# Two of four sums of weight blocks formed by adding transfers, and more pairs of k-tiles in seven block products

## Chip, cores and metric

The kernel runs on one core of one Trainium2 chip. The metric is the device time of one execution in microseconds (us). Three runs of the kernel before took 2425.48, 2425.89 and 2425.93 us; the median, 2425.89, is the time before.

## The reference, cut to what matters

A decoder trunk of two layers works on a residual stream x of 256 tokens by 2048, in float32. Layer 0 mixes tokens by retention in 8 heads, layer 1 by latent attention in 16 heads, and a SwiGLU network of width 5632 follows each. Every sub-layer is `x = x + rms_norm(f(rms_norm(x)))`.

```python
def swiglu(x, w_gu, w_down):
    gate, up = jnp.split(x @ w_gu, [D_FF], axis=-1)
    return (jax.nn.silu(gate) * up) @ w_down

for i in range(DEPTH):
    h = rms_norm(x, norm_mix_pre[i])
    h = retention(h, ...) if i % 2 == 0 else mla(h, ...)
    x = x + rms_norm(h, norm_mix_post[i])
    h = rms_norm(x, norm_ffn_pre[i])
    x = x + rms_norm(swiglu(h, ffn_w_gu[i], ffn_w_down[i]), norm_ffn_post[i])
```

Nearly all the work is the products of 256 tokens with large weight matrices, which are read from memory once.

## The kernel before

**Products.** A k-tile is 128 rows of a weight matrix. A group (`group`) forms 256 tokens by 1024 output columns in four PSUM banks: two token tiles t by two column halves c of 512. Its loop runs over the k-tiles: 16 in the retention's input projection (4 groups of q and k, named rqk, and 8 of v and gate, rvg) and in the gate/up projection (11 groups in each of two layers, gu); the down projection (dn, 44 k-tiles), the retention's output (rto, 32) and the attention's output (mlo, 16) have two groups each, called halves, in `closing`.

**Precision.** Each float32 operand is split (`split`) into a rounded part hi, a cast on ACT (line 203), and a rest lo, a subtraction on DVE (line 204). A product is three matmuls: hi by hi, hi by lo, lo by hi. So an ordinary pair of k-tiles has 2 tiles x 2 t x 2 c x 3 = 24 matmuls of 512 columns.

**Seven products.** For the pairs named in GU_SEVENS, DN_SEVENS, RTO_SEVENS and RET_SEVENS the four blocks of the pair's weights (two k-tiles by two halves, b00, b01 in the first tile and b10, b11 in the second) and the four blocks of activations are multiplied in Strassen's way (Winograd's form): seven products in place of eight, so 21 matmuls in place of 24 (`seven`). They need four sums of activation blocks (`left_sums`, made once and used by all groups of a stage) and four sums of weight blocks, made for each pair in each group (`right_sums`, lines 246 to 249):

    t1 = b00 + b01     t3 = b01 + b11     t2 = t1 + b11     t4 = t2 + b10

Each is an addition of 512 columns on DVE. The sums t1 and t3 lie in the tile ta, t2 and t4 in tb; both are split like weights. b01 itself isn't split, since no product uses it alone. After the last seven of a group, `combine` takes four products out of four extra banks, and `add` adds them to the group's banks.

**What sets the order.** The program is written in the order of the loops, and a scheduler puts each engine's instructions in an order of its own when the program is built; on the chip each engine keeps that order and waits at an instruction until its operands and its buffer are there. A tile with a tag has as many buffers as `bufs` says: raw weights (`raw`) four, hi and lo (`whi`, `wlo`) five each. A buffer is given to the next tile when the last reader of the old one has finished: whi and wlo are freed by PE, raw by DVE. All weights are loaded by SP's queue, 512 KB for a k-tile. `later` and `step` put small pieces of work (transposes, norms) a number of k-tiles ahead in the next group; in gate/up two sets of four transposes stand between pair 0 and pair 1, and ACT copies their results to aT.

Of the kernel before, what the change touches and what calls it, by code (L numbers as in the profile page):

```python
# [33 lines left out]
GU_SEVENS = (2, 3, 5)  # L34
DN_SEVENS = (2, 5, 8, 11, 14, 17)
RTO_SEVENS = (2, 6, 10)
RET_SEVENS = (2, 4)
# [19 lines left out]
def trunk(  # L57
# [153 lines left out]
    def weights(load, parts, name):  # L211

        raw = wp.tile([P, 1024], F32, tag="raw", bufs=RAW, name=f"{name}_raw")
        load(raw)
        hi = wp.tile([P, 1024], F32R, tag="whi", bufs=WB, name=f"{name}_hi")
        lo = wp.tile([P, 1024], F32R, tag="wlo", bufs=WB, name=f"{name}_lo")
        for a, n, g in parts:
            split(hi[:, a : a + n], lo[:, a : a + n], raw[:, a : a + n], g)
        return hi, lo, raw
# [18 lines left out]
    def right_sums(raw0, raw1, name):  # L238

        b00, b01 = raw0[:, 0:512], raw0[:, 512:1024]  # L240
        b10, b11 = raw1[:, 0:512], raw1[:, 512:1024]
        res = {}
        ta = tp7.tile([P, 1024], F32, tag="tsum", bufs=2, name=f"{name}_ta")
        tb = tp7.tile([P, 1024], F32, tag="tsum", bufs=2, name=f"{name}_tb")
        t1, t3, t2, t4 = ta[:, 0:512], ta[:, 512:1024], tb[:, 0:512], tb[:, 512:1024]
        nc.vector.tensor_add(out=t1, in0=b00, in1=b01)
        nc.vector.tensor_add(out=t3, in0=b01, in1=b11)
        nc.vector.tensor_add(out=t2, in0=t1, in1=b11)
        nc.vector.tensor_add(out=t4, in0=t2, in1=b10)  # L249
        for both, src, n in ((ta, (1, 3), "a"), (tb, (2, 4), "b")):  # L250
            hi = wp.tile([P, 1024], F32R, tag="whi", bufs=WB, name=f"{name}_t{n}hi")
            lo = wp.tile([P, 1024], F32R, tag="wlo", bufs=WB, name=f"{name}_t{n}lo")
            split(hi, lo, both)
            for i, k in enumerate(src):
                sl = slice(i * 512, (i + 1) * 512)
                res[k] = hi[:, sl], lo[:, sl]
        return res

    def group(
        lhs, kts, load, name, lead=2, skew=0, tail=0, banks=None, between=None, sevens=(), left=None  # L260
    ):

# [50 lines left out]
        def seven(p, final):  # L313
            k0, k1 = 2 * p, 2 * p + 1

            def b(kt, c):
                return lambda: tuple(x[:, c * 512 : (c + 1) * 512] for x in w[kt][:2])
# [13 lines left out]
        def combine():  # L331
            def kept(n):
                return wp.tile([P, 512], F32, tag="mv", bufs=3, name=f"{name}_mv{n}")

            m1, u, v = kept(0), kept(1), kept(2)
# [4 lines left out]
            x = tp7.tile([P, 1024], F32, tag="tsum", bufs=2, name=f"{name}_mx")[:, 0:512]  # L340
# [65 lines left out]
    def tile_load(w, g, name, halves=0):  # L406
# [3 lines left out]
        def load(kt, first_half=False):  # L410
            n = 512 if kt < halves or first_half else 1024

            def dma(raw):
                for a in range(0, 1024, 512 if kt < halves else 1024):
                    m = 512 if kt < halves else 1024
                    nc.sync.dma_start(out=raw[:, a : a + m], in_=w[g, kt, :, a : a + m])

            parts = [(a, n, None) for a in range(0, 512 if first_half else 1024, n)]
            return weights(dma, parts, f"{name}_w{kt}")
# [6 lines left out]
    hT = hp.tile([P, DT, 2, NT, P], F32R, tag="hT", name="hT")  # L426
# [4 lines left out]
    def watched(sevens, tiles):  # L431

        made, held = {}, {}

        def seen(t, k0, n, part):
            for p in sevens:
                if k0 <= 2 * p < k0 + n:
                    held[t, p] = part[:, 2 * p - k0], part[:, 2 * p - k0 + 1]
                    if (1 - t, p) in held:
                        f, hi, lo = tiles(len(made))  # L440
# [4 lines left out]
        return made  # L445

    def norm_piece(t, i, ssq, col):
# [6 lines left out]
        ks = slice(k0, k0 + n)  # L454
        part = wp.tile([P, 512], F32, tag="mv", bufs=3, name=f"hx{t}{i}")
# [5 lines left out]
        split(hT[:, ks, 0, t, :], hT[:, ks, 1, t, :], part)  # L461
# [11 lines left out]
    def h_lhs(kt, t, c):  # L473
        return hT[:, kt, 0, t, :], hT[:, kt, 1, t, :]

    rx_next = [None] * NT

# [13 lines left out]
    yg = sb.tile([P, NT, D], F32, tag="yg", name="yg")  # L491

    def closing(act, kts, w, g_post, col, name, skew=4, sevens=(), sums=None):


        last = col is None
        ssq = [small(4, "ssq", 4, f"{name}_ssq{t}") for t in range(NT)]
# [3 lines left out]
        def parted(half, b):  # L501
# [5 lines left out]
            if b in sevens:  # L507
# [4 lines left out]
        def update(t, k0, n):  # L512
            sl = slice(k0 * P, (k0 + n) * P)
            nc.vector.scalar_tensor_tensor(
                out=xs[:, t, sl], in0=yg[:, t, sl], scalar=r[t], in1=xs[:, t, sl],
# [13 lines left out]
        parted(0, 0)  # L529
        for half in range(2):  # L530
            gp = sb.tile([P, 1024], F32, tag="gp", name=f"{name}_gp")
            nc.sync.dma_start(
                out=gp, in_=g_post[half * 1024 : (half + 1) * 1024].partition_broadcast(P)
            )

# [6 lines left out]
            def load(kt, *first_half):  # L542
# [5 lines left out]
                return slices(kt, *first_half)  # L548
# [21 lines left out]
            def scaled(banks, t):  # L570
                for c in range(2):
                    col = half * 2 + c
                    nc.vector.tensor_tensor(  # L573
                        out=yg[:, t, col * 512 : (col + 1) * 512], in0=banks[t][c],
                        in1=gp[:, c * 512 : (c + 1) * 512], op=ALU.mult,
                    )

            def first_done(banks):
# [10 lines left out]
                lhs, kts, load, f"{name}{half}", skew=skew if half else 0, tail=2 if half else 0,  # L589
# [632 lines left out]
```

## Time and profile before

| What | Value |
|---|---|
| profiled execution, its time | 2426.96 us |
| its span | 2425.2 us |
| mean granted TensorE clock | 0.998 |
| bytes moved, mean rate | 463.78 MB, 191 GB/s |
| a rqk group, and a gate/up group, on PE | 46.59 us, 42.70 us |
| 1024-column cast on ACT, subtraction on DVE | 1.05 us, 1.22 us |

The span is the time from the first to the last instruction. The page of the profile gives each engine's busy time, the DMA queues and the chain of work that ended last; views of the trace give instructions grouped by line, waits, issues of transfers with their time to landing, and timelines. In a row of instructions, `gu_w_lo<-gu_w_raw,gu_w_hi` names the tile written and the tiles read. The time of an instruction includes the tail in which its writes are confirmed; the next one on its engine starts before that.

### The profile page before, as it was taken

Reading aid. Unit: us, or ns where it says so; the run is one execution under the profiler, and the core shown is the slowest. Engines: PE = TensorE matmul, PEld = TensorE weight load, DVE = VectorE, ACT = ScalarE, POOL = GpSimd, SP = SyncE. Lnnn points to the kernel's source line nnn. Section 1 sums busy time; section 2 is a strip of 40 time slices with the busy share of each in tenths; the row PEclk is TensorE's granted clock in tenths of the full one; section 3 lists DMA queues with packets and bytes.
Section 4 is the critical chain, followed back from the end, with each engine's and each line's share of the span. In section 5 each row is a group of like instructions: output and inputs, shape, how many; then the busy total and the mean of one; then the engine's idle time right before and its main releaser. Section 6 shows DMA issues by size and latency. Waiting matters only on the chain.

```text
span 2425.2 us, 30883 instructions
## 1 busy us (share of the span) xinstructions
PE 2412.2 (99%) x10972; PEld 1993.3 (82%) x10972; DVE 2080.2 (86%) x2865; ACT 1409.8 (58%) x1882; POOL 26.2 (1%) x38
## 2 busy tenths in 40 slices
PE   9999999999999999999999999999999999999998
PEld 7888888888888888888888888888888888888886
DVE  7888888888878998888999997876889889899997
ACT  5454555555656655555565665655655565556664
POOL 0000000000000000000000000000000000000000
PEclk9999999999999999999999999999999999999999
DMA  7556556555665565666656655336556656566654
GB/s 255 173 194 194 180 184 200 171 190 191 198 212 189 183 206 190 199 204 191 203 190 209 207 198 163 123 132 199 184 182 202 197 192 212 183 204 199 204 198 162
DMA packets 129612, 463.78 MB, mean 191 GB/s; under 512 B 14640, under 2 KB 15024, under 8 KB 129456
## 3 DMA queue, kind: packets, MB, share of 16 engines
q1 hardware_dynamic: 129456, 461.80, 58.5%
q8 instruction: 86, 1.41, 0.2%
q14 instruction: 70, 0.57, 0.1%
HBM read 459.64 MB, written 2.10 MB: 190 GB/s over the span
## 4 chain that ended last, share of the span: by engine, by line
PE 96%; DVE 2%; DMA 1%; issue 1%; ACT 0%; SPq 0%; DVEq 0%; POOLq 0%; POOL 0%; ACTq 0%
PE gu_b L399 31%; PE dn_b L399 14%; PE rvg_b L399 12%; PE gu_m L399 7%; PE rto_b L399 6%; PE rqk_b L399 6%; PE mlo_b L399 4%; PE q L399 3%; PE dn_m L399 2%; PE rvg_m L399 2%; PE mc_b L399 2%; PE ftp L816 1%; PE rqk_m L399 1%; PE rto_m L399 1%; PE ry L749 1%; PE htp L451 1%
## 5 line engine op out<-in xcount | busy, mean ns | idle before, releaser
L399 PE MATMUL gu_b<-gu_w_hi,hT 128*128 128x512 f32 x1976 | 564.0, 392 | 0.0
L203 ACT CAST gu_w_hi<-gu_w_raw 128x1024 fp32r<-128x1024 f32 (+1 forms) x352 | 342.4, 979 | 238.2 <-PE gu_b L399 163.8
L204 DVE TENSOR_TENSOR gu_w_lo<-gu_w_raw,gu_w_hi 128x1024 fp32r<-128x1024 f32 (+1 forms) x352 | 392.3, 1130 | 47.4 <-ACT gu_w_hi L203 45.4
L399 PEld LDWEIGHTS gu_b<-gu_w_hi,hT 128*128 128x128 f32 x1976 | 366.7, 188 | 75.0 <-DVE hT L204 0.9
L399 PE MATMUL gu_b<-gu_w_lo,hT 128*128 128x512 f32 x988 | 310.1, 390 | 0.0
L203 ACT CAST dn_w_hi<-dn_w_raw 128x1024 fp32r<-128x1024 f32 (+1 forms) x176 | 172.8, 993 | 99.6 <-DMA dn_w_raw<-w_down 51.9
L399 PE MATMUL rvg_b<-rvg_w_hi,hT 128*128 128x512 f32 x800 | 227.0, 391 | 0.0
L399 PEld LDWEIGHTS gu_b<-gu_w_lo,hT 128*128 128x128 f32 x988 | 185.2, 188 | 39.5 <-DVE gu_w_lo L204 0.6
L204 DVE TENSOR_TENSOR dn_w_lo<-dn_w_raw,dn_w_hi 128x1024 fp32r<-128x1024 f32 (+1 forms) x176 | 196.3, 1148 | 8.6 <-ACT dn_w_hi L203 7.9
L203 ACT CAST rvg_w_hi<-rvg_w_raw 128x1024 fp32r<-128x1024 f32 (+1 forms) x128 | 127.3, 1000 | 117.6 <-PE rvg_b L399 93.6
L204 DVE TENSOR_TENSOR rvg_w_lo<-rvg_w_raw,rvg_w_hi 128x1024 fp32r<-128x1024 f32 (+1 forms) x128 | 145.2, 1154 | 36.1 <-ACT rvg_w_hi L203 34.9
L399 PEld LDWEIGHTS rvg_b<-rvg_w_hi,hT 128*128 128x128 f32 x800 | 149.0, 188 | 30.3
L399 PE MATMUL dn_b<-dn_w_hi,dn_ah 128*128 128x512 f32 x536 | 169.7, 390 | 0.1
L399 PE MATMUL dn_b<-dn_w_lo,dn_ah 128*128 128x512 f32 x536 | 169.0, 389 | 0.0
L399 PE MATMUL dn_b<-dn_w_hi,dn_al 128*128 128x512 f32 x536 | 168.9, 389 | 0.0
L399 PE MATMUL rvg_b<-rvg_w_lo,hT 128*128 128x512 f32 x400 | 124.8, 390 | 0.0
L399 PE MATMUL rqk_b<-rqk_w_hi,hT 128*128 128x512 f32 x428 | 121.0, 394 | 1.1 <-ACT rqk_w_hi L203 0.9
L399 PEld LDWEIGHTS dn_b<-dn_w_hi,dn_al 128*128 128x128 f32 x536 | 100.6, 188 | 20.9
L399 PEld LDWEIGHTS dn_b<-dn_w_lo,dn_ah 128*128 128x128 f32 x536 | 100.6, 188 | 20.9
L399 PEld LDWEIGHTS dn_b<-dn_w_hi,dn_ah 128*128 128x128 f32 x536 | 100.3, 188 | 21.0 <-DVE yg L573 0.4
L203 ACT CAST gu_w_tbhi<-gu_w_tb 128x1024 fp32r<-128x1024 f32 x60 | 63.1, 1052 | 86.7 <-DVE gu_w_tb L249 47.4
L204 DVE TENSOR_TENSOR gu_w_tblo<-gu_w_tb,gu_w_tbhi 128x1024 fp32r<-128x1024 f32 x60 | 73.5, 1225 | 36.8 <-ACT gu_w_tbhi L203 34.3
(442 smaller groups left out, 4763.9 us busy)
## 6 DMA issues: line engine op xcount, KB each, us to landing
gu_w_raw<-w_gu SPq DMA_DIRECT2D x352, 512.0 KB, 4.3
dn_w_raw<-w_down SPq DMA_DIRECT2D x176, 512.0 KB, 4.4
rvg_w_raw<-ret_vg SPq DMA_DIRECT2D x128, 512.0 KB, 4.4
rto_w_raw<-ret_out SPq DMA_DIRECT2D x64, 512.0 KB, 4.4
rqk_w_raw<-ret_qk SPq DMA_DIRECT2D x63, 512.0 KB, 4.4
mlo_w_raw<-mla_out SPq DMA_DIRECT2D x32, 512.0 KB, 3.5
uq_w_raw<-mla_up SPq DMA_DIRECT2D x32, 448.0 KB, 3.4
mc_w_raw<-mla_c SPq DMA_DIRECT2D x16, 512.0 KB, 4.4
```

What stands on the lines that cost most here:

```text
L203: nc.scalar.copy(out=hi, in_=src)
L204: nc.vector.tensor_sub(out=lo, in0=src, in1=hi.bitcast(F32))
L399: nc.tensor.matmul(out, e[2](), e[3](), start=bank not in begun, stop=ends[bank, bank in added] == n, skip_group_check=bank in added,)
L451: nc.tensor.transpose(tp[:, j * P : (j + 1) * P], xs[:, t, (k0 + j) * P : (k0 + j + 1) * P], ident)
L749: nc.tensor.matmul(y, left, right, start=n == 0, stop=n == len(terms) - 1)
L816: nc.tensor.transpose(tp[:, b * P : (b + 1) * P], a[:, b * P : (b + 1) * P], ident)
```

## The change

1. **Weight sums by adding transfers.** `right_sums` is gone. `begin_seven` loads b00, and b10 with b11, by SP's queue into a tile `raws` (2 buffers); ACT copies b00 and b11 side by side into the first half of a tile of four sums (line 250); then a transfer issued by POOL reads b01 twice from memory and adds it to both (line 251), which makes t1 and t3. `split_seven` forms t2 and t4 by two additions on DVE (lines 259 and 260) and splits b00 (512 columns), b10 with b11, t1 with t3, and t2 with t4 (1024 each). b01 has no load of its own.
2. **When it begins.** `ahead` lays out the pairs of a stage in one sequence and calls `begin_seven` in the loop five pairs before the seven is due (AHEAD), across the border of a group.
3. **More sevens.** GU_SEVENS goes from three to four pairs of eight (20 groups), RET_SEVENS from two to three (11 groups), RTO_SEVENS from three in each half to four and five of sixteen, DN_SEVENS from six in each half to seven and eight of twenty-two (two layers).
4. **Memory.** To make room, the tile yg becomes two tiles of tag y8, whose two buffers also hold the sums of the retention and of gate/up; hT becomes four quarters of tag h8, whose four buffers also hold the sums of the closing projections; fa, gp, sf and the attention's p share or lose buffers; gp is loaded at k-tile 8 of a half; the DMA scratch goes from 2048 to 1024.

```diff
-GU_SEVENS = (2, 3, 5)
-DN_SEVENS = (2, 5, 8, 11, 14, 17)
-RTO_SEVENS = (2, 6, 10)
-RET_SEVENS = (2, 4)
+GU_SEVENS = (1, 2, 4, 5)
+DN_SEVENS = ((4, 6, 9, 11, 13, 16, 18), (1, 4, 6, 9, 11, 13, 16, 18))
+RTO_SEVENS = ((4, 7, 9, 11), (1, 4, 7, 9, 11))
+RET_SEVENS = (2, 4, 5)
+
+AHEAD = 5
...
-    def right_sums(raw0, raw1, name):
...
+    def begin_seven(w, g, p, pool, tag, bufs, name):
+        k0, k1 = 2 * p, 2 * p + 1
+        raw = tp7.tile([P, 3, 512], F32, tag="raws", bufs=2, name=f"{name}_r")
+        nc.sync.dma_start(out=raw[:, 0, :], in_=w[g, k0, :, 0:512])
+        nc.sync.dma_start(
+            out=raw[:, 1:3, :], in_=w[g, k1].rearrange("p (i c) -> p i c", i=2)
+        )
+        sums = pool.tile([P, 4, 512], F32, tag=tag, bufs=bufs, name=f"{name}_t")
+        nc.scalar.copy(out=sums[:, 0:2, :], in_=raw[:, 0:3:2, :])
+        nc.gpsimd.dma_start(
+            out=sums[:, 0:2, :], in_=w[g, k0, :, 512:1024][:, None, :].to_broadcast([P, 2, 512]),
+            accum_op=ALU.add,
+        )
+        return raw, sums
+
+    def split_seven(raw, sums, name):
+        nc.vector.tensor_add(out=sums[:, 2, :], in0=sums[:, 0, :], in1=raw[:, 2, :])
+        nc.vector.tensor_add(out=sums[:, 3, :], in0=sums[:, 2, :], in1=raw[:, 1, :])
+        res = []
+        for n, src in (("0", raw[:, 0:1, :]), ("1", raw[:, 1:3, :]), ("a", sums[:, 0:2, :]), ("b", sums[:, 2:4, :])):
+            hi = wp.tile([P, 1024], F32R, tag="whi", bufs=WB, name=f"{name}_{n}hi")
+            lo = wp.tile([P, 1024], F32R, tag="wlo", bufs=WB, name=f"{name}_{n}lo")
+            m = 512 * src.shape[1]
+            split(hi[:, 0:m], lo[:, 0:m], src.rearrange("p i c -> p (i c)"))
+            res.append((hi, lo))
...
+    def ahead(seq, begin):
+        at = [(n, p) for n, (pairs, _) in enumerate(seq) for p in range(pairs)]
...
+        for n, (_, sevens) in enumerate(seq):
+            for p in sevens:
+                m, q = at[max(first[n, p] - AHEAD, 0)]
+                def fn(n=n, p=p):
+                    begun[n][p] = begin(n, p)
+                todo[m].setdefault(q, []).append(fn)
+        return list(zip(todo, begun))
...
         def load_one(kt):
             step()
-            w[kt] = load(kt, True) if kt % 2 == 0 and kt // 2 in sevens else load(kt)
+            if kt % 2:
+                for fn in early[0].get(kt // 2, ()):
+                    fn()
+            if each is not None:
+                each(kt)
+            if kt // 2 not in sevens:
+                w[kt] = load(kt)
 
         def sums(p):
-            w["t", p] = right_sums(w[2 * p][2], w[2 * p + 1][2], f"{name}_w{p}")
+            w[2 * p], w[2 * p + 1], w["t", p] = split_seven(*early[1][p], f"{name}_w{p}")
...
-    yg = sb.tile([P, NT, D], F32, tag="yg", name="yg")
+    def y_tile(name):
+        return sb.tile([P, D], F32, tag="y8", bufs=2, name=name)
```

How the orders change is shown for ACT and DVE in the gate/up projection of layer 0, group 5 of 11, around its last seven. In the names `gu0_5_w10` is k-tile 10 of that group; before, `w5_ta` and `w5_tb` are the sums of pair 5 (k-tiles 10 and 11). After, `gu0_5_5_r` are the raws and `gu0_5_5_t` the sums of pair 5, and `w5_0`, `w5_1`, `w5_a`, `w5_b` its four split tiles (b00; b10 and b11; t1 and t3; t2 and t4); `gu0_6_1` is pair 1 of the next group.

Before, ACT's queue at this place holds casts alone:

```order
L203 CAST gu0_5_w9_hi_8588<-gu0_5_w9_raw_8586 128x1024
L203 CAST gu0_5_w10_hi_8606<-gu0_5_w10_raw_8604 128x512
L203 CAST gu0_5_w11_hi_8612<-gu0_5_w11_raw_8610 128x1024
L203 CAST gu0_5_w5_tahi_8622<-gu0_5_w5_ta_8616 128x1024
L203 CAST gu0_5_w5_tbhi_8626<-gu0_5_w5_tb_8617 128x1024
L203 CAST gu0_5_w12_hi_8662<-gu0_5_w12_raw_8660 128x1024
```

After, ACT's queue there reads:

```order
L205 CAST gu0_5_w4_0hi_8711<-gu0_5_4_r_8488 128x512
L250 COPY gu0_5_5_t_8546<-gu0_5_5_r_8543 128x1024
L205 CAST gu0_5_w4_1hi_8715<-gu0_5_4_r_8488 128x1024
L205 CAST gu0_5_w4_ahi_8719<-gu0_5_4_t_8491 128x1024
L205 CAST gu0_5_w4_bhi_8723<-gu0_5_4_t_8491 128x1024
L205 CAST gu0_5_w5_0hi_8756<-gu0_5_5_r_8543 128x512
L250 COPY gu0_6_1_t_8706<-gu0_6_1_r_8703 128x1024
L205 CAST gu0_5_w5_1hi_8760<-gu0_5_5_r_8543 128x1024
L205 CAST gu0_5_w5_ahi_8764<-gu0_5_5_t_8546 128x1024
L205 CAST gu0_5_w5_bhi_8768<-gu0_5_5_t_8546 128x1024
```

The copy of pair 5's raws now stands among pair 4's casts, and the copy for the next group's pair 1 stands ahead of three of pair 5's four casts.

Before, DVE's queue around pair 5 reads:

```order
L246 TENSOR_TENSOR gu0_5_w5_ta_8616<-gu0_5_w10_raw_8604 128x512
L204 TENSOR_TENSOR gu0_5_w8_lo_8571<-gu0_5_w8_raw_8568,gu0_5_w8_hi_8570 128x1024
L204 TENSOR_TENSOR gu0_5_w9_lo_8589<-gu0_5_w9_raw_8586,gu0_5_w9_hi_8588 128x1024
L204 TENSOR_TENSOR gu0_5_w10_lo_8607<-gu0_5_w10_raw_8604,gu0_5_w10_hi_8606 128x512
L247 TENSOR_TENSOR gu0_5_w5_ta_8616<-gu0_5_w10_raw_8604,gu0_5_w11_raw_8610 128x512
L204 TENSOR_TENSOR gu0_5_w11_lo_8613<-gu0_5_w11_raw_8610,gu0_5_w11_hi_8612 128x1024
L248 TENSOR_TENSOR gu0_5_w5_tb_8617<-gu0_5_w5_ta_8616,gu0_5_w11_raw_8610 128x512
```

After, DVE's queue there reads:

```order
L206 TENSOR_TENSOR gu0_5_w4_1lo_8716<-gu0_5_4_r_8488,gu0_5_w4_1hi_8715 128x1024
L206 TENSOR_TENSOR gu0_5_w4_alo_8720<-gu0_5_4_t_8491,gu0_5_w4_ahi_8719 128x1024
L259 TENSOR_TENSOR gu0_5_5_t_8546<-gu0_5_5_t_8546,gu0_5_5_r_8543 128x512
L260 TENSOR_TENSOR gu0_5_5_t_8546<-gu0_5_5_t_8546,gu0_5_5_r_8543 128x512
L206 TENSOR_TENSOR gu0_5_w4_blo_8724<-gu0_5_4_t_8491,gu0_5_w4_bhi_8723 128x1024
L206 TENSOR_TENSOR gu0_5_w5_0lo_8757<-gu0_5_5_r_8543,gu0_5_w5_0hi_8756 128x512
L206 TENSOR_TENSOR gu0_5_w5_1lo_8761<-gu0_5_5_r_8543,gu0_5_w5_1hi_8760 128x1024
L206 TENSOR_TENSOR gu0_5_w5_alo_8765<-gu0_5_5_t_8546,gu0_5_w5_ahi_8764 128x1024
```

Two of four additions are left, and the first of them, which waits for POOL's adding transfer, stands ahead of the last split of pair 4.

More of the change, by code (lines that the diff above doesn't have):

```diff
@@ L259, in group @@
     def group(
-        lhs, kts, load, name, lead=2, skew=0, tail=0, banks=None, between=None, sevens=(), left=None
+        lhs, kts, load, name, lead=2, skew=0, tail=0, banks=None, between=None, sevens=(), left=None,
+        early=({}, {}), each=None,
     ):
@@ L529, in closing @@
         parted(0, 0)
+        if not last:
+            begin_input()
         for half in range(2):
[L531 to L534, printed above, removed]
             def lhs(kt, t, c):
```

159 lines of the change are left out of this document (91 added, 68 removed).

## The prediction

> **What bounds the kernel now.** I read the page first, then the stretches of one group, the waits, the chain in order of time, and the timelines of ACT and DVE.
>
> ```profile
> PE 2412.2 (99%) x10972; PEld 1993.3 (82%) x10972; DVE 2080.2 (86%) x2865; ACT 1409.8 (58%) x1882; POOL 26.2 (1%) x38
> q1 hardware_dynamic: 129456, 461.80, 58.5%
> PE 96%; DVE 2%; DMA 1%; issue 1%; ACT 0%; SPq 0%; DVEq 0%; POOLq 0%; POOL 0%; ACTq 0%
> 854.33:897.03 42.70, 42.70 (x193) 35.07 (x192) 38.59 (x50) 24.39 (x27) 0.00 (x0) 1.00 0.61 197
> 854.33 18.37 PE gu_b L399 x81
> 872.70 0.44 PE ftp L816 x4
> ```
>
> PE is never idle. One gate/up group lasts 42.70 us, all of it PE, at full clock. 81 matmuls take 18.37 us, so one takes 0.2268 us; a transposing set of four takes 0.44. What takes matmuls away shortens the time, as long as PE's operands still come in time.
>
> ```profile
> ACT gu_w_hi L203 <- PE gu_b L399: 163.8, 140, 3.1
> ACT rvg_w_hi L203 <- PE rvg_b L399: 93.6, 64, 3.5
> ```
>
> ACT's casts mostly wait for PE: with five buffers of whi, a cast waits until PE has finished the tile five earlier. So ACT and DVE run ahead of PE by no more than those buffers, and it is in this lead that every new wait has to fit.
>
> **What the change takes off PE.** The splits of the b sums count the pairs in seven products.
>
> ```profile
> L204 DVE TENSOR_TENSOR gu_w_tblo<-gu_w_tb,gu_w_tbhi 128x1024 fp32r<-128x1024 f32 x60 | 73.5, 1225 | 36.8 <-ACT gu_w_tbhi L203 34.3
> L204 DVE TENSOR_TENSOR dn_w_tblo<-dn_w_tb,dn_w_tbhi 128x1024 fp32r<-128x1024 f32 x24 | 29.3, 1222 | 5.3 <-ACT dn_w_tbhi L203 5.2
> L204 DVE TENSOR_TENSOR rvg_w_tblo<-rvg_w_tb,rvg_w_tbhi 128x1024 fp32r<-128x1024 f32 x16 | 19.6, 1223 | 7.2 <-ACT rvg_w_tbhi L203 7.2
> L204 DVE TENSOR_TENSOR rto_w_tblo<-rto_w_tb,rto_w_tbhi 128x1024 fp32r<-128x1024 f32 x6 | 7.3, 1224 | 4.6 <-ACT rto_w_tbhi L203 4.6
> L204 DVE TENSOR_TENSOR rqk_w_tblo<-rqk_w_tb,rqk_w_tbhi 128x1024 fp32r<-128x1024 f32 x6 | 7.3, 1223 | 4.4 <-ACT rqk_w_tbhi L203 4.4
> ```
>
> By the new tables the 60 become 80 (20 groups, 3 to 4), the 24 become 30, rvg and rqk's 22 become 33 (11 groups, 2 to 3), rto's 6 become 9: 112 become 152. A pair has 24 matmuls, in seven products 21. 40 x 3 x 0.2268 = **27.2 us less PE**.
>
> **What it does to DVE, ACT and DMA.** Steps between starts, back to back:
>
> ```profile
> 1027.92 0.69 DVE L339 TENSOR_TENSOR gu_mv<-gu_m,gu_mv 128x512 f32<-128x512 f32 x1
> 1028.52 0.68 DVE L341 TENSOR_TENSOR gu_mx<-gu_m,gu_mv 128x512 f32<-128x512 f32 x1
> 1029.12 1.22 DVE L204 TENSOR_TENSOR gu_w_lo<-gu_w_raw,gu_w_hi 128x1024 fp32r<-128x1024 f32 x1
> 1030.25 1.29 DVE L346 TENSOR_TENSOR gu_b<-gu_b,gu_mv 128x512 f32<-128x512 f32 x2
> 1010.67 1.06 ACT L203 CAST gu_w_tbhi<-gu_w_tb 128x1024 fp32r<-128x1024 f32 x1 [0.30 <-PE gu_m L399]
> 1022.23 1.05 ACT L203 CAST gu_w_hi<-gu_w_raw 128x1024 fp32r<-128x1024 f32 x1 [0.53 <-PE gu_b L399]
> 1023.18 0.58 ACT L336 COPY gu_mv<-gu_m 128x512 f32<-128x512 f32 x1
> 1023.66 1.05 ACT L203 CAST gu_w_hi<-gu_w_raw 128x1024 fp32r<-128x1024 f32 x1
> ```
>
> DVE steps 0.60 for 512 columns and 1.13 for 1024 (1.23 until a reader may go on), ACT 0.95 for 1024 (1.06 for a reader) and 0.48 for 512; a cast starts 0.30 after PE's release. DVE loses 112 x 4 adds and gets 152 x 2, and each of the 40 new pairs has 1.5 more splits of 1024: -86 + 68 = -18 us. ACT gets 152 copies of 1024 and 60 more casts: 212 x 0.95 = 201 us, so some 66% busy. Both stay under PE: no cost in throughput. A pair read 1 MB and now reads 0.75 MB and adds 0.5 MB: 152 x 0.25 is 40 MB more, and the adding transfers must read their 80 MB of destination too. At 461.8 MB for 58.5% that makes 74%: not full, no cost by itself. The halves of yg, hT in quarters, fa in one buffer, the later load of gp and ACT's other copies touch nothing that PE waits for: nothing.
>
> **The added wait.** The raws have two buffers. So the load for one seven starts only when DVE has split the raws of the second seven before it, whatever the five pairs say: in gate/up (1, 2, 4, 5) pair 5's follows pair 2's, in the retention's (2, 4, 5) too. Then come the load (L), ACT's copy, and POOL's adding transfer (X, to its landing), all before DVE's add at line 259. And ACT's queue holds the next group's copy ahead of pair 5's casts. In the down and out projections four or five pairs, over 20 us, lie between: nothing there.
>
> Gate/up, in us from the start of pair 2 on PE. Pair 0 ends at -5.64 (pair 1 is 4.76, two transposing sets 0.88). From -5.34 ACT does pair 2's first half cast 0.48, an aT copy 0.48, pair 4's sums copy 0.95, another aT copy 0.48, pair 2's second cast 1.06: -1.89. DVE's split: -0.66. Pair 5's load lands at L - 0.66, ACT's copy ends at L + 0.4, the adding transfer lands at L + X + 0.4. On DVE's queue pair 5's two adds (1.2) stand ahead of pair 4's b split (1.23): it ends at L + X + 2.83 = C. Only then may ACT copy into the sums buffer that this split read (the next group's pair 1), and behind that copy stand pair 5's casts. Copy 0.95, second cast 1.06, then DVE's 1.13 + 1.13 + 1.23: the b split of pair 5 ends at C + 5.5. PE needs it at pair 5's eighth matmul: 4.76 + 5.44 + 4.76 + 7 x 0.2268 = 16.55. So **PE waits L + X - 8.22** in each of 20 groups.
>
> Retention. Pair 1 is ordinary, so pair 2's second split ends at -4.2 (w0's buffer at -6.5, cast 1.06, split 1.23). The adding transfer lands at L + X - 3.15; an add and pair 4's second split (0.6 + 1.23) wait for it, and that split frees the raws for the next group's pair 2, whose load lands at 2L + X - 1.32 and whose copy stands in ACT's queue ahead of all of pair 5's casts. From there 0.95 + 0.48 + 1.06 + 1.13 + 1.13 + 1.23 = 5.98; PE needs it at the seventh matmul, 14.96 + 6 x 0.2268 = 16.32. **PE waits 2L + X - 11.66** in each of 11 groups.
>
> L and X come from the issues to landing and POOL's instruction:
>
> ```profile
> gu_w_raw<-w_gu SPq DMA_DIRECT2D x352, 512.0 KB, 4.3
> mlo_w_raw<-mla_out SPq DMA_DIRECT2D x32, 512.0 KB, 3.5
> rto_gp<-g_mix_post SPq DMA_DIRECT2D x2, 512.0 KB, 5.1
> L120 POOL TENSOR_TENSOR grs<-bve,mhalf 128x1 f32<-128x1 f32 x16 | 8.8, 548 | 535.3 <-DVE bve L755 535.3
> ```
>
> L = 4.3, from the same tensor in the same stage. No transfer of POOL's and none that adds is in the trace. Below, X is 3.5, a load in the quietest stage; above, two loads one after the other, 8.6. I take 5.1 + 0.55 = 5.65: the transfer nearest in kind reads a repeated source for 512 KB in 5.1, and POOL spends 0.55 on its smallest instruction. Then gate/up waits 1.73 x 20 = 34.6 and the retention 2.59 x 11 = 28.5: 63.1. Sum: -27.2 + 63.1 = **+35.9**. The profiled execution took 2426.96 (span 2425.2), 1.1 over the median; from the median 2425.9 it is **2462**. At X = 8.6: 4.68 x 20 + 5.54 x 11 = 154.5, 2553. At L = X = 3.5 both waits are gone: 2425.9 - 27.2 = 2398.7.
>
> By the Trainium skill (Collectives: The Full Stack, The bandwidth ceiling) an add in the DMA engines costs a second source read and no more; with the 2.0 us and 436 GB/s that DMA: Bandwidth & Descriptors (Anatomy of one DMA) gives for a transfer from this queue, my estimate is X = 4.4, waits of 9.6 and 14.7, and 2423. No run here shows it yet.
>
> **Rivals.**
> 1. The adding transfers come in time: 2399 to 2420, faster. For it: DVE is 18 us lighter, the chain needs only L + X under 8.2, and a quiet load takes 3.5; the bounds of X include it, and at L = X = 4.3 it is 7.6 + 13.6 - 27.2, 2420. Against it: a load here takes 4.3 at a DMA share of 0.61, which rises. It decides from X under 4.3. Chance 0.34.
> 2. POOL is held off by DVE: slower than forecast. DVE is 86% busy; if POOL may write its transfer only between DVE's instructions and misses three of 1.13, X is 9.0: waits 5.08 x 20 + 5.94 x 11 = 167, 2566. Against it: nothing shows POOL waiting for a DVE that it does not depend on. Chance 0.08. The skill (SBUF — State Buffer, Who interferes with whom) has such a lock for DVE's two-port modes, and excepts the tensor-tensor form that nearly all rows here have; no run here shows it.
> 3. The waits just eat the gain: they sum to 22 to 32, X about 4.5: within 0.2%. Chance 0.07.
>
> **How the numbers follow.** Forecast (X from 4.7 to 7.8, 2431 to 2530): 0.51. About 0.2%, 5 us, is what a measurement can tell from no change. Faster 0.34 (rival 1), same 0.07 (rival 3), slower 0.51 + 0.08 = 0.59. The range goes from 2400, nearly the whole gain, to 2530; left out are the full gain's edge and rival 2, under 0.2. The forecast's own range is 2431 to 2530.
>
> **What would show it.** Right: PE idle of 1 to 3 us once in each gate/up and rvg group, at pair 5's first matmuls, released by ACT or DVE; ahead of it ACT idle before the copy at line 250, DVE idle at line 259 behind the adding transfer; down and out projections as full as now. Wrong: gate/up groups of 42.0 us with PE full mean that X is short (rival 1); the issue-to-landing row of the adding transfers gives X itself, and over 8 us rival 2. Stalls at pair 4, or in the down projection, would mean that my queue table is wrong and not X.

## The result, and the profile after

The changed kernel takes 2639.27 us (median of four runs, 2638.91 to 2644.91) against 2425.91 before: 1.0885 times as long, with a 95% interval of 1.0866 to 1.0904. Forecast were 2462, and at most 2530. The sign was right; of 213 us the forecast had 36.

The changed kernel's row of cores (span, mean granted clock):

```profile
core 0: 2637.1 us, clock 0.967
```

Its page (busy time, share and instructions of each engine; then the two weight queues, SP's and POOL's, with packets, MB and share of the 16 DMA engines):

```profile
PE 2484.1 (94%) x10852; PEld 2001.1 (76%) x10852; DVE 2069.5 (78%) x2861; ACT 1589.2 (60%) x2126; POOL 209.6 (8%) x190
q1 hardware_dynamic: 129456, 421.95, 46.0%
q0 software_dynamic: 41344, 79.70, 17.9%
```

PE has 120 matmuls less, as it should, and yet is busy for 72 us more. The clock tells most of it: a mean of 0.967, in stretches at 0.50 and at 1.00, is 174 us at half speed (2 x 0.033 x 2637.1), where before it was some 10. Over the whole kernel DVE, ACT and the DMA engines are all further from full than PE. Where the time went in the profiled execution of each run, from the first matmul of a stage to the first of the next (gate/up and down twice, one for each layer; the last down projection to its last matmul; e9's profiled execution is 7 us under its median, the others are within 3):

| stage, us | before | changed | e1 | e2 | e3 | e5 | e7 | e9 | e12 |
|---|---|---|---|---|---|---|---|---|---|
| rqk | 190.8 | 222.5 | 199.7 | 215.1 | 190.4 | 198.9 | 209.7 | 192.0 | 189.6 |
| rvg | 362.9 | 390.0 | 368.9 | 382.0 | 362.3 | 371.3 | 376.3 | 361.0 | 362.9 |
| rto | 173.9 | 182.9 | 179.4 | 175.4 | 175.5 | 177.0 | 177.6 | 175.4 | 173.6 |
| gate/up 0 | 474.3 | 525.0 | 526.6 | 565.7 | 468.1 | 526.0 | 511.7 | 515.7 | 467.4 |
| down 0 | 233.5 | 252.9 | 250.5 | 238.3 | 236.7 | 240.9 | 240.3 | 242.6 | 232.6 |
| gate/up 1 | 474.4 | 525.8 | 525.1 | 561.0 | 469.0 | 524.3 | 511.1 | 512.6 | 469.9 |
| down 1 | 231.9 | 252.8 | 248.2 | 240.1 | 236.4 | 243.4 | 240.4 | 241.8 | 231.9 |

In the changed kernel every stage with adding transfers lost. The waits of the changed kernel (who waited for whom: total us, times, longest) name the places:

```profile
ACT dn_t L250 <- DMA dn_r<-w_down: 101.9, 30, 5.6
ACT gu_t L250 <- DVE gu_w_blo L206: 83.2, 17, 6.0
ACT gu_t L250 <- DMA gu_r<-w_gu: 80.8, 38, 5.4
DVE gu_t L259 <- DMA gu_t<-w_gu: 72.0, 20, 5.1
PEld gu_m L441 <- DVE gu_w_blo L206: 64.4, 42, 3.5
```

ACT stands at its copies, DVE at its additions, and PE then at the last split of a seven. The timelines of a gate/up group (start, duration, engine; in brackets the idle time before and what ended it), with PE's pair 2 beginning at 1004.36:

```profile
1002.47 1.23 DVE L206 TENSOR_TENSOR gu_w_1lo<-gu_r,gu_w_1hi 128x1024 fp32r<-128x1024 f32 x1 [1.99 <-ACT gu_w_1hi L205]
1004.36 0.39 PE L441 MATMUL gu_m<-gu_w_0hi,hT 128*128 128x512 f32 x1
1009.87 1.05 ACT L250 COPY gu_t<-gu_r 128x1024 f32<-128x1024 f32 x1 [2.65 <-DMA gu_r<-w_gu]
1011.33 1.21 POOL L251 DMA_DIRECT2D gu_t<-w_gu  x1 [8.69 <-ACT gu_t L250]
1018.02 0.69 DVE L259 TENSOR_TENSOR gu_t<-gu_t,gu_r 128x512 f32<-128x512 f32 x1 [3.75 <-DMA gu_t<-w_gu]
1019.35 1.22 DVE L206 TENSOR_TENSOR gu_w_blo<-gu_t,gu_w_bhi 128x1024 fp32r<-128x1024 f32 x1
1020.63 0.50 PE L441 MATMUL gu_m<-gu_w_blo,sh 128*128 128x512 f32 x1 [2.28 <-DVE gu_w_blo L206]
1020.60 1.05 ACT L250 COPY gu_t<-gu_r 128x1024 f32<-128x1024 f32 x1 [5.17 <-DVE gu_w_blo L206]
1022.37 0.63 PE L441 MATMUL gu_m<-gu_w_0lo,hT 128*128 128x512 f32 x1
1022.80 0.63 PE L441 MATMUL gu_m<-gu_w_0hi,hT 128*128 128x512 f32 x1
1024.55 0.80 PE L441 MATMUL gu_m<-gu_w_bhi,sh 128*128 128x512 f32 x1 [1.12 <-ACT gu_w_bhi L205]
```

This is the chain of the prediction, link by link: pair 2's split ends at 1003.70, pair 5's raws are there at 1009.87 (L = 6.17), ACT's copy ends at 1010.92, the adding transfer has landed at 1018.02 (X = 7.10), and only behind pair 5's additions comes pair 4's last split, with PE waiting. The copy for the next group then starts after ACT has stood for 5.17 us, and pair 5's casts behind it. From 1022.37 to 1022.80 is 0.43 us, not 0.2268: PE runs at half speed. Windows of the same group (length, busy time of PE, PEld, DVE, ACT, POOL; then granted clock, DMA share and GB/s), first while pair 5's raws and the adding transfer are under way, then three of 3.41 us:

```profile
1003.70:1009.87 6.17, 6.17 (x29) 5.12 (x28) 6.17 (x7) 3.26 (x4) 0.00 (x0) 1.00 1.00 268
1015.00:1018.02 3.02, 3.02 (x15) 2.44 (x13) 0.00 (x1) 0.44 (x1) 0.00 (x0) 1.00 1.03 274
1018.42:1021.83 3.41, 1.20 (x5) 1.03 (x6) 2.72 (x4) 1.23 (x2) 0.00 (x0) 1.00 0.08 30
1021.83:1025.24 3.41, 2.29 (x6) 1.28 (x6) 2.61 (x3) 3.41 (x4) 1.22 (x1) 0.50 0.35 55
1025.24:1028.65 3.41, 3.41 (x10) 2.56 (x9) 3.09 (x4) 1.63 (x3) 0.00 (x0) 0.50 1.02 250
```

While PE stands still the DMA engines are at 0.08, for the transfer has landed and PE waits for DVE's additions and the split behind them. But in the links ahead of that they are full: 1.00 while the raws come, 1.03 in the last 3 us of the adding transfer. Over the 20 groups the share is 1.00 in the median during the load and 0.82 from the copy's end to the addition. So the mean of 64% (46.0 and 17.9) hides that the DMA engines are full just where the chain waits for them. And the window in which PE was idle for 2.2 us is followed by two at half clock.

### The profile page after: what moved, and what is told of

Read it like the earlier page. It is cut to its first block, busy times and chain, and to the rows that moved or that the text cites. A ratio compares the mean times of both kernels' runs of the same rounds, so it can differ in the third digit from the quotient of the medians.

```text
span 2637.1 us, 31117 instructions
## 1 busy us (share of the span) xinstructions
PE 2484.1 (94%) x10852; PEld 2001.1 (76%) x10852; DVE 2069.5 (78%) x2861; ACT 1589.2 (60%) x2126; POOL 209.6 (8%) x190
## 3 DMA queue, kind: packets, MB, share of 16 engines
q0 software_dynamic: 41344, 79.70, 17.9%
## 4 chain that ended last, share of the span: by engine, by line
issue 57%; PE 22%; DMA 8%; DVE 6%; POOL 5%; ACT 2%; SPq 0%; POOLq 0%; ACTq 0%; DVEq 0%
PE rvg_b L441 4%; PE mlo_b L441 3%; POOL gu_t L251 3%; PE dn_b L441 3%; PE q L441 3%; DMA ret_t<-ret_vg 2%; DMA ret_r<-ret_vg 2%; PE gu_b L441 1%; PE mc_b L441 1%; PE rto_b L441 1%; POOL dn_t L251 1%; PE rvg_m L441 1%; DMA dn_t<-w_down 1%; DVE rvg_w_1lo L206 1%; PE dn_m L441 1%
## 5 line engine op out<-in xcount | busy, mean ns | idle before, releaser
L441 PE MATMUL gu_b<-gu_w_hi,hT 128*128 128x512 f32 x1536 | 421.6, 390 | 0.0
L206 DVE TENSOR_TENSOR gu_w_lo<-gu_w_raw,gu_w_hi 128x1024 fp32r<-128x1024 f32 x192 | 231.9, 1217 | 13.4 <-ACT gu_w_hi L205 12.7
L205 ACT CAST gu_w_hi<-gu_w_raw 128x1024 fp32r<-128x1024 f32 x192 | 198.0, 1049 | 70.9 <-PE gu_m L441 26.7
L250 ACT COPY gu_t<-gu_r 128x1024 f32<-128x1024 f32 x80 | 83.9, 1049 | 166.8 <-DVE gu_w_blo L206 83.2
L206 DVE TENSOR_TENSOR gu_w_1lo<-gu_r,gu_w_1hi 128x1024 fp32r<-128x1024 f32 x80 | 97.9, 1224 | 106.5 <-ACT gu_w_1hi L205 106.5
L251 POOL DMA_DIRECT2D gu_t<-w_gu x80 | 97.5, 1218 | 879.6 <-ACT gu_t L250 868.1
L206 DVE TENSOR_TENSOR dn_w_lo<-dn_w_raw,dn_w_hi 128x1024 fp32r<-128x1024 f32 x116 | 138.0, 1218 | 23.6 <-ACT dn_w_hi L205 23.4
L205 ACT CAST dn_w_hi<-dn_w_raw 128x1024 fp32r<-128x1024 f32 x116 | 117.7, 1047 | 28.7 <-PE dn_b L441 8.1
L205 ACT CAST gu_w_bhi<-gu_t 128x1024 fp32r<-128x1024 f32 x80 | 83.8, 1048 | 56.2 <-issue 49.0
L206 DVE TENSOR_TENSOR gu_w_blo<-gu_t,gu_w_bhi 128x1024 fp32r<-128x1024 f32 x80 | 97.6, 1220 | 22.1 <-ACT gu_w_bhi L205 22.1
```

What stands on the lines that cost most here:

```text
L205: nc.scalar.copy(out=hi, in_=src)
L206: nc.vector.tensor_sub(out=lo, in0=src, in1=hi.bitcast(F32))
L250: nc.scalar.copy(out=sums[:, 0:2, :], in_=raw[:, 0:3:2, :])
L251: nc.gpsimd.dma_start(out=sums[:, 0:2, :], in_=w[g, k0, :, 512:1024][:, None, :].to_broadcast([P, 2, 512]), accum_op=ALU.add,)
L441: nc.tensor.matmul(out, e[2](), e[3](), start=bank not in begun, stop=ends[bank, bank in added] == n, skip_group_check=bank in added,)
```

## The experiments

Theory "latency" at first: the chain is as forecast, only L and X are longer. Against it "traffic": copies and adding transfers slow everything. With e2 a third came up, "queue": the order on DVE and ACT puts the addition and the copy of a later seven ahead of the splits that PE needs next.

**e1: nobody reads what is added.**

```
-        nc.vector.tensor_add(out=sums[:, 2, :], in0=sums[:, 0, :], in1=raw[:, 2, :])
+        nc.vector.tensor_add(out=sums[:, 2, :], in0=raw[:, 0, :], in1=raw[:, 2, :])
...
-        for n, src in (("0", raw[:, 0:1, :]), ("1", raw[:, 1:3, :]), ("a", sums[:, 0:2, :]), ("b", sums[:, 2:4, :])):
+        for n, src in (("0", raw[:, 0:1, :]), ("1", raw[:, 1:3, :]), ("a", sums[:, 2:4, :]), ("b", sums[:, 2:4, :])):
```

> All loads, ACT copies and adding transfers of the changed kernel stay; only nobody reads what the transfers have added (t1 and t3 are left out: t2 is formed from b00 and b11, and t1 with t3 is split from t2 and t4). Theory 'latency' (PE waits for the chain raws free, load, copy, adding transfer, add; the changed kernel shows 6.2 us for the load and 7.1 from the copy's end to the landing in one group): the stalls of gate/up and of the retention's groups go, those in the down projection where ACT stands at its copy for the raws stay (24 us), some 10 in rqk: about 2440, 2410 to 2470. Theory 'traffic' (the adding transfers and copies slow every load, ACT and DVE): they are all still there, so over 2560.

Measured: 2584.7 us. The number lies where "traffic" put it, over 2560, but the stages don't: the retention recovers 44 of its 59 us, the output and down projections 2 to 5 each, gate/up nothing. The waits show what the edit did besides: with no transfer to wait for, the scheduler put the addition still earlier on DVE, where it now waits for the raws themselves:

```profile
DVE gu_t L259 <- DMA gu_r<-w_gu: 103.4, 38, 5.6
```

So the run doesn't separate latency from traffic; it shows that the place of the waiting instruction matters.

**e2: the tables of before, with adding transfers** (four lines of tables).

> The changed kernel with the tables of before: 112 sevens in place of 152, all with adding transfers. PE's work is that of before. Latency: in gate/up pair 5 again follows pair 2's raws, but pair 4 between them is ordinary and no seven's last split stands behind a wait that late; in the down projection three pairs lie between sevens: 2426 to 2460. Traffic: 112 of 152 parts of the 240 us that the transfers cost, 177, on 2426: about 2603.

Measured: 2661.8 us, more than with 152 sevens, and outside both expectations. A cost that grows with the number of transfers would be less by a quarter, so traffic in that sense falls as the main cause; and the latency theory in its first form falls too, since the sevens 2, 3 and 5 should have had time. DVE's timeline, and two rows of PE's:

```profile
1106.76 0.69 DVE L259 TENSOR_TENSOR gu_t<-gu_t,gu_r 128x512 f32<-128x512 f32 x1 [2.93 <-DMA gu_t<-w_gu]
1107.37 1.22 DVE L206 TENSOR_TENSOR gu_w_blo<-gu_t,gu_w_bhi 128x1024 fp32r<-128x1024 f32 x1
```

```profile
1108.64 0.50 PE L441 MATMUL gu_m<-gu_w_blo,sh 128*128 128x512 f32 x1 [0.81 <-DVE gu_w_blo L206]
1115.35 0.39 PE L441 MATMUL gu_m<-gu_w_0hi,hT 128*128 128x512 f32 x1
```

The addition is pair 5's; PE begins pair 5 at 1115.35, 8.6 us later. But the split behind it on DVE is pair 3's, and PE stands waiting for that one.

**e3: the sevens without the transfers.** The four sums are made on DVE as before (`right_sums`), with the new tables and the new memory.

> All 152 sevens of the changed kernel, its memory too, but without begin_seven: the pair's weights are loaded and the four sums added on DVE as before. If only the adding transfers cost time, PE's 27 us come through, less what DVE now lacks: a gate/up group has 38.59 + 4.1 = 42.7 us on DVE against 42.0 on PE, 14 us over 20 groups at the least: 2410 to 2440. If more sevens cost time by themselves (their splits on ACT and DVE), over 2500.

Measured: 2423.28 us, 0.9988 times before (0.9979 to 0.9998), as the first expectation has it. So the 40 sevens do no harm on the whole, and the 216 us between this and the changed kernel belong to the adding transfers with what goes with them: the copies, the buffers of the raws and the order. Gate/up gains 6.2 and 5.4 us of 6.8 to be had; the down projections lose 3.2 and 4.5.

**e4: PE's stalls filled.**

```
+        def filler():
+            for _ in range(9):
+                nc.tensor.matmul(
+                    ms[6], fill[:, 0:P], fill, start=False, stop=False, skip_group_check=True,
+                )
...
+                if i == 6 and fill is not None and p in sevens[2:]:
+                    plan.append(("do", filler))
```

> The changed kernel with nine matmuls on zeros (they add zero to the sixth product's bank) put ahead of the sixth product in pairs 4 and 5 of each gate/up group, where PE stands still for some 2.3 and then 1.3 us: 360 matmuls, 82 us of PE work more. Theory 'clock' (a stall of over about 1.9 us in a window of 3.41 us makes the granted clock 0.5 for the next window, which costs about 0.9 us in each gate/up group beyond the waits): the clock stays at 1.00 in gate/up and the time falls by some 17 us, to 2622. Rival (the halved clock costs nothing, since PE waits anyway, or comes from something else): the work is hidden at best, 2639, or added where it isn't, up to 2700.

Measured: 2717.8 us, 79 more than the changed kernel, nearly all of the 82 added, and over both ranges. The clock did recover (0.982, so 98 us at half speed in place of 174; in gate/up 20 in place of 109), which speaks for PE's standing still as what halves it. But new stalls came at the ordinary pairs behind. The row of cores, then waits of PE's weight loads:

```profile
core 0: 2718.7 us, clock 0.982
```

```profile
PEld gu_b L449 <- issue: 28.2, 20, 3.1
PEld gu_b L449 <- DVE gu_w_lo L206: 28.0, 35, 1.1
```

The added matmuls also changed the scheduler's order on the other engines. What the halved clock costs alone stays open.

**e5: the additions behind the last split.** An edge that orders issue on DVE and adds no wait:

```
+    before = [None]
...
-        nc.vector.tensor_add(out=sums[:, 2, :], in0=sums[:, 0, :], in1=raw[:, 2, :])
-        nc.vector.tensor_add(out=sums[:, 3, :], in0=sums[:, 2, :], in1=raw[:, 1, :])
+        with tc.issue_after(before[0]) if before[0] is not None else nullcontext():
+            nc.vector.tensor_add(out=sums[:, 2, :], in0=sums[:, 0, :], in1=raw[:, 2, :])
+            nc.vector.tensor_add(out=sums[:, 3, :], in0=sums[:, 2, :], in1=raw[:, 1, :])
...
+        before[0] = nc.cur_bb.bb.instructions[-1]
```

> The changed kernel, with one thing more: an order edge (no wait) on DVE puts the two additions of a seven behind the last split of the seven before it, where now they stand ahead of it. Same transfers, copies, tables and buffers. Theory 'queue' (DVE stands at the addition of a later seven for a transfer that takes 7.1 us from the copy's end, while the split that PE needs next stands behind it; the copy into the buffer which that split frees, and the casts behind the copy, come late in turn): in gate/up the stall of pair 4 goes, that of pair 5 shrinks to about 0.9 us in place of 5.9 with the halved clock, 100 us over 20 groups; the retention loses some 40 and the down projection 10: about 2490, 2460 to 2540. Theory 'traffic': nothing changes but the order, over 2610.

Measured: 2569.1 us, 70 less, between the two ranges. The same transfers, so their traffic alone can't be the cause of these 70. The retention gains 42, the output and down projections 27, gate/up nothing, where 100 had been expected. There the wait went to ACT, where the copy for the next group stands ahead of pair 5's casts. ACT's timeline, then a row of the waits:

```profile
972.36 1.05 ACT L250 COPY gu_t<-gu_r 128x1024 f32<-128x1024 f32 x1 [4.91 <-DMA gu_r<-w_gu]
```

```profile
PEld gu_m L445 <- ACT gu_w_bhi L205: 72.6, 20, 4.9
```

**e6: copies later in the closing projections** (e5, and there the copy is issued after the first cast of the seven before).

> As e5, and in the down and output projections ACT's copy of a seven's raws stands behind the first cast of the seven before it (it stood a pair of k-tiles or so earlier, and ACT stood at it for 102 us in the down projections, 5 at most each time, since the raws were still on their way). Theory 'queue': those stalls of dn_b (24 us, released by ACT's casts of ordinary k-tiles) go: some 25 us under e5. Rival (ACT's wait there is hidden, and PE's stalls in dn come from the adding transfer): within 5 us of e5.

Measured: 2584.5 us, 15 more than e5, so both expectations fail. ACT's wait fell from 90.9 us to 26.4 as meant, and the down projections grew by 7.7 and 2.9, the retention's output by 5.4: a later copy is a later transfer, for which DVE then stands. The wait in e5, then two in e6:

```profile
ACT dn_t L250 <- DMA dn_r<-w_down: 90.9, 30, 5.0
```

```profile
DVE dn_t L274 <- DMA dn_t<-w_down: 56.6, 22, 4.9
ACT dn_t L254 <- DMA dn_r<-w_down: 26.4, 14, 5.6
```

The biggest row in the changed kernel's waits, ACT at the down projection's copies, was therefore not what to mend first.

**e7: the transfer without the adding.** The sums t1 and t3 are left out.

```
-            accum_op=ALU.add,
```

> The changed kernel with POOL's transfer as a plain copy (b01 is written in place of b00 + b01 and b11 + b01; the sums are left out). It shows what of the 6.5 us from issue to landing is the adding. A packet of 2 KB takes 84 ns in a plain transfer and 178 in an adding one, 16 of them for each engine are 1.5 us: if the adding is the cost, 5.0 us to landing and a time of about 2590. If the issue from POOL is, 6.3 and about 2630.

Measured: 2553.6 us, one run, still less than the first expectation; the order on every queue is the changed kernel's. Issue to landing in the changed kernel, then, in this one, POOL's group of instructions (mean ns of one), issue to landing, and the queue:

```profile
gu_r<-w_gu SPq DMA_DIRECT2D x80, 512.0 KB, 5.8
gu_t<-w_gu POOLq DMA_DIRECT2D x80, 512.0 KB, 6.5
```

```profile
L251 POOL DMA_DIRECT2D gu_t<-w_gu x80 | 58.1, 726 | 876.3 <-ACT gu_t L250 870.5
```

```profile
gu_r<-w_gu SPq DMA_DIRECT2D x80, 512.0 KB, 4.7
gu_t<-w_gu POOLq DMA_DIRECT2D x80, 512.0 KB, 4.3
```

```profile
q0 software_dynamic: 21888, 79.70, 9.2%
```

Adding costs 2.2 us of landing time, and the loads beside it become 1.1 shorter when it is gone. POOL's instruction takes 0.73 in place of 1.22. The queue's time on the DMA engines is halved: 17.9% of 2637.1 is 472 us, 9.2% of 2551.8 is 235. During the raws' load in gate/up the engines are then at 0.76 in place of 1.00 (medians of 20 groups). So some 86 us hang on the adding, and part of them on the loads that it lengthens.

**e8: as e3, with gate/up's old table.**

> Sums on DVE and no adding transfers, as in e3; the new tables in the retention, its output and the down projections (132 sevens), the old one in gate/up, where DVE has 90% of a group. PE loses 20 x 3 x 0.2268 = 13.6 us against before: 2412 if DVE (85% busy in those stages, some 4.1 us more for each added seven) stays under PE there, 2408 to 2418. If the longer queues of DVE stall PE as they seem to in e3 (2423, where 2399 was to be had), 2418 to 2430.

Measured: 2434.5 us, 1.0036 (1.0022 to 1.0049). Both expectations fail: added sevens gain nothing in the retention (0.4 us less and 1.4 more) and lose 2.6 and 3.1 in the down projections. Where PE's saving goes there stays open.

**e9: the next group's copy behind this group's last cast** (e5, and in gate/up and the retention the copy and the adding transfer of a group's first seven are traced behind the last cast of the group before, with `issue_after`).

> As e5, and in gate/up and the retention ACT's copy for the first seven of the next group stands behind the last cast of the last seven of this group, where it stood ahead of three of its casts. In e5 the gate/up stages are no shorter than in the changed kernel (526 and 524 us): there ACT stands 4.9 us at that copy for raws still on their way, with pair 5's casts behind it. Theory 'queue': pair 4 stays without a stall and pair 5's goes from about 5 us to 1.2: some 45 us less in each gate/up stage, 10 in the retention: about 2470, 2450 to 2510. If each order edge only moves the wait to the next place, over 2540.

Measured: 2533.3 us, 36 less than e5, between the two ranges. The retention is now at 553.0 us for both parts, where before had 553.7 with 7.5 us more of PE's work. Gate/up gained 10 and 12 of the 45 expected in each layer; there DVE and ACT wait in turn for what has only just been begun:

```profile
985.21 1.05 ACT L254 COPY gu_t<-gu_r 128x1024 f32<-128x1024 f32 x1 [4.12 <-DMA gu_r<-w_gu]
992.95 0.69 DVE L274 TENSOR_TENSOR gu_t<-gu_t,gu_r 128x512 f32<-128x512 f32 x1 [2.21 <-DMA gu_t<-w_gu]
```

**e12: DVE sums, the new table in gate/up alone.**

> Sums on DVE as in e3, the new table in gate/up alone, the old ones elsewhere. In e3 the gate/up stages were 5.4 and 6.2 us shorter than before of 6.8 to be had, and the other stages as long or longer. If that is by their own tables, only gate/up's gain stays: 2426 - 11.6 = 2414 to 2418. If the stages around lose by the new memory (mc 1.7, down projections 3 to 4 each), 2418 to 2424. Over 2426 would mean that four sevens on DVE are too many.

Measured: 2414.03 us, 0.9950 times before (0.9938 to 0.9963), as the first expectation has it: faster than both kernels, by 12 us. The new memory is e8's, so what e8 loses in the other stages is not due to it. Of 100 us in gate/up, PE is busy for all and DVE for 98.92 at a clock of 1.00:

```profile
1000.00:1100.00 100.00, 100.00 (x449) 82.39 (x448) 98.92 (x119) 62.63 (x69) 0.00 (x0) 1.00 0.63 200
```

Most of gate/up's 13.6 us, and 12 of the 27.2 that the change was after, could be had with DVE full there and no adding transfer at all.

**e13 and e14: three buffers for the raws on top of e9, and its measure.**

```
-    RAW, WB = 4, 5
+    RAW, WB = 3, 5
...
+        turn[0] = (turn[0] + 1) % 3 if third is not None else 0
+        if turn[0] == 2:
+            raw = third.tile([P, 3, 512], F32, tag="raws3", bufs=1, name=f"{name}_r")
```

> As e9, and in the gate/up and down projections a seven's raws have three buffers in place of two (every third tile lies in the stage's own memory); for the room there are three raw buffers for ordinary k-tiles in place of four. ACT's copy of pair 5 now stands one cast earlier and need not wait for its raws; the rest of the order is e9's. Theory 'buffers' (what is left in e9, 41 and 38 us in the gate/up stages and 9 in each down projection, is the chain of a load of 6 to 7 us and a transfer of 7 that only starts when the second seven before is split): pair 5's sums land some 4 us earlier, and most of gate/up's 80 us go: about 2465, 2450 to 2490, if e14 shows that the room costs nothing. Theory 'traffic' (adding transfers, loads and engines disturb one another): as e14.

> As e9, with three raw buffers for ordinary k-tiles in place of four and nothing else: the measure for e13. Ordinary pairs lose one tile of lead: 2530 to 2550.

Measured: e13 2535.3, e14 (of this edit only the first two lines) 2597.7; both are over their ranges. The room is not free, it costs 64 us over e9; the third buffer gives 62 back by the medians, and 50 in the profiled executions, 35 of them in gate/up, where some 80 had been expected. So the lead of two buffers is part of the cause. Two variants of the changed kernel that took the room elsewhere as well, e10 and e11, gave no time.

**e15: the larger DMA scratch, on e13.**

```
-dynamic_dma_scratch_size=1024
+dynamic_dma_scratch_size=2048
```

> As e13, with the DMA scratch at 2048 as before the change (1024 in the change); the order on every queue is e13's. In e13 pair 5's adding transfer is issued 6.8 us after pair 4's, as soon as that has landed, and POOL stands for up to 6 us at it; it then lands 9.6 us after its copy. Theory 'one at a time' (with the small scratch POOL can't issue a second adding transfer while one is under way): POOL no longer waits, pair 5's sums land 7 to 8 us after the copy, and 1.5 to 2.5 us of the 2 that PE waits in each group go, some 30 to 40 us with the halved clock: about 2500. Rival (the transfers share the same engines and only finish later each): the first takes 8 to 9 us as well, and the time stays within 10 us of 2535.

Measured: 2547.9 us, 13 more than e13, so neither expectation holds as it was put. POOL's wait for the transfer before, then the transfers' issue to landing, first of e13:

```profile
POOL gu_t L259 <- DMA gu_t<-w_gu: 159.7, 23, 8.9
```

```profile
gu_t<-w_gu POOLq DMA_DIRECT2D x80, 512.0 KB, 8.2
```

And of e15:

```profile
POOL gu_t L259 <- DMA gu_t<-w_gu: 37.3, 7, 5.5
```

```profile
gu_t<-w_gu POOLq DMA_DIRECT2D x80, 512.0 KB, 8.6
```

The scratch did hold POOL back: in e13 no transfer of gate/up was issued before the one ahead of it had landed, in e15 29 of 79 were. But issued earlier, they take longer: in the retention two transfers 4.29 us apart landed 6.5 and 9.3 us after their issue. For the transfers of pairs 1 and 2 in gate/up the second is issued 5.7 us sooner after the first than in e13 and lands 3.0 sooner (medians), and yet the kernel gained nothing. So the theory "one at a time" has the wait right and its price wrong. Close together, adding transfers hold each other up. What is left in gate/up in e13 (23 and 28 us over before) is of that kind or of the lead; the runs don't divide it further.

## Why the prediction was right or wrong

Three steps failed. L and X, the load and the adding transfer in the chain, were mis-sized: 4.3 and 5.65 in the forecast, 6.2 and 7.1 in gate/up. "Nothing there" for the closing projections was wrong: they lost 55 us. And "not full, no cost by itself" took the DMA engines by their mean, though they are full while the chain waits for its load. Nor was there a term for a slower PE behind a stall. The forecast's sum was -27.2 + 63.1. The same terms measured, as growth of the stages plus the PE work taken out of them:

| | forecast | measured |
|---|---|---|
| gate/up, 20 groups | 34.6 | 50.7 + 51.4 + 13.6 = 115.7 |
| retention, 11 groups | 28.5 | 31.7 + 27.1 + 7.5 = 66.3 |
| output and down projections | 0 | 9.0 + 19.4 + 20.9 + 6.1 = 55.4 |

Of the 177 us that the forecast lacks, 101 are L and X put into its own two formulas (103 and 61 in place of 63.1, below), 55 the closing projections, some 18 what the formulas leave in gate/up and the retention, and 3 lie in a stage between.

**PE's 27.2 us.** Right: 120 matmuls fewer, and e12 gains 11.4 us in its gate/up stages where 13.6 are to be had.

**No cost in throughput.** Right for DVE and ACT, and for the DMA engines only in the mean: they are at 64%, not 74, or 69% of the time before, since the span is longer. The same 79.70 MB take 472 us of the engines when they add and 235 when they don't. The Trainium skill (Collectives: The Full Stack, The bandwidth ceiling) gives an add the cost of a second source read; the trace agrees. What the step left out is where that time falls: the engines are at 1.00 while pair 5's raws come, and that load is the link of the chain that grew most over the forecast.

**The chain in gate/up.** The mechanism was right: with L = 6.17 and X = 7.10, L + X - 8.22 is 5.05 us in the group shown; with L and X read from the timelines of all 20 groups the waits sum to 103, and 115.7 were lost. Both sizes were wrong. X was taken from a load plus POOL's smallest instruction (5.65), and L as a load of before (4.3), though a seven's raws are 768 KB in two transfers and run beside an adding one: 5.8 from issue to landing in the median, and 4.7 in e7, where nothing adds. The bounds moved X alone, so the upper end, 2553, was no bound. The stall at pair 4, which the forecast called a sign of a wrong table, is one that the table did not test: pair 4's last split ends at L + X + 2.83 = 16.1 after pair 2's start, and PE needs it at 4.76 + 5.44 + 16 x 0.2268 = 13.83, so it is 2.3 late, and 2.28 are in the row; at the forecast's L and X it was in time. But the formula describes one state and is no slope: e5 took away its first link and gate/up stayed, as the next wait stood right behind.

**The retention.** The mechanism was right here too. In the forecast's chain the next group's copy stands ahead of pair 5's casts, and so it does in an rvg group, on ACT, with PE waiting for one of those casts:

```profile
309.15 1.05 ACT L250 COPY ret_t<-ret_r 128x1024 f32<-128x1024 f32 x1 [4.47 <-DMA ret_r<-ret_vg]
313.62 0.50 PE L441 MATMUL rvg_m<-rvg_w_bhi,rxh 128*128 128x512 f32 x1 [1.38 <-ACT rvg_w_bhi L205]
```

With the issue rows of the changed kernel (4.5 and 6.5 + 0.4 in rvg, 5.4 and 8.5 + 0.4 in rqk) 2L + X - 11.66 is 4.2 x 8 + 8.0 x 3 = 58; read from the timelines of the ten groups that have a next one it is 61, of the 66 measured. That it was the order on DVE and ACT is shown: e9, with the same transfers, brings the stage back to the time before, which is 59 of the 66; the 7 of PE's saving stay lost.

**"Nothing there" in the down projection.** This step was wrong in kind. It measured the distance in pairs of k-tiles, over 20 us, and not where on the queues the waiting instructions stand. Timelines of ACT, DVE and PE in the changed kernel's first down projection:

```profile
1422.08 1.05 ACT L250 COPY dn_t<-dn_r 128x1024 f32<-128x1024 f32 x1 [5.02 <-DMA dn_r<-w_down]
1423.55 1.99 ACT L205 CAST dn_w_hi<-dn_w_raw 128x1024 fp32r<-128x1024 f32 x2
1430.03 0.69 DVE L259 TENSOR_TENSOR dn_t<-dn_t,dn_r 128x512 f32<-128x512 f32 x1 [2.44 <-DMA dn_t<-w_down]
1435.38 0.80 PE L441 MATMUL dn_m<-dn_w_blo,sh 128*128 128x512 f32 x1 [3.29 <-DVE dn_w_blo L206]
```

A later seven's copy and addition stand ahead of casts and splits that PE needs first. e5 takes 12.0 and 9.4 us off these stages by moving the additions behind those splits.

**The clock.** The sum had no term for it. PE was busy for 142 of the 174 us at half speed, so its matmuls took up to 71 us longer there; less of that counts where PE would have waited for the chain anyway. What the formulas leave of gate/up and the retention, some 18 us, is an estimate of what came on top in these stages. How much of the 213 us the clock is, the runs don't show, since e4 changed the order too.

**The rivals.** The first (in time) needed X under 4.3; even the transfer without adding takes 4.3 from its issue. The second, at 2566, is nearest in its number, and not for its reason: POOL starts 0.41 us after the copy's end in the median, and is not held off by DVE. The third is out.

## What to carry to other kernels

A step that waits for a transfer costs what stands behind it on its engine, not what it itself delays: look in the order for the instruction of a later tile that waits ahead of one of the next tile, on each engine, and move it behind; here that alone (e9) gave back 106 of the 240 us by which the changed kernel stands over the time before less its 27.2 us of PE work. Bound every link of a serial chain, not only the new one, since a longer transfer lengthens the loads beside it, and read the share of the DMA engines in the stretch of that link, not over the kernel. And before moving work to another engine to make room, try the change with the work left where it is: e12, with DVE 99% full in gate/up, beat everything else.

## What was not expected of the hardware

**Short stalls halve the clock.** Over the changed kernel there are 32 stretches at half clock, of 3.41 us or multiples, on a fixed grid. In the window of that grid right ahead of each, PE was idle for 1.59 to 3.41 us, in 29 of the 32 for 1.81 to 2.97; in the windows that none followed, for at most 1.75. The Trainium skill (TensorE: Matmul & The Clock Gate, What's actually happening) has that free-running window of 3413 ns; its rule against idle gaps over 3.4 us (HAM oscillation — how this bites in real kernels) is too mild here: gaps of 2.3 us were enough.

**A larger scratch shifts the queue more than it shortens it.** At 1024 POOL waits for the transfer before, at 2048 the transfers overlap, and of the 5.7 us by which the second is issued sooner behind the first in gate/up's pairs 1 and 2 only 3.0 are left at its landing, which then comes 10.7 us after its issue in place of 8.2.
